# A hybrid decoder layer on one core: the order of input loads, weight casts and forget gates in the first stage

## The chip, the core and the metric

The kernel runs on one core of one Trainium2 chip. The metric is the device time of one execution in microseconds (us), as the median of several runs. The profile is of one further execution.

## The reference

One layer of a hybrid decoder works on 2,048 prompt tokens and 32 sample tokens (eight sequences of four), of width 1,024, in float32:

```python
h = rmsnorm(x, g_pre)
proj = h @ w_in                    # q, k, v, z_a, r, glu, z_b, g_a, g_b
log_a = log_sigmoid(r @ w_a_up + b_a_up) / 16
o, s_new = gla_chunked(q, k, v, log_a, s0)        # S_t = diag(alpha_t) S_{t-1} + k_t^T v_t ; o_t = q_t S_t
y_a = (rmsnorm(o, g_gla) * silu(z_a)) @ w_a_out
u = glu_a * sigmoid(glu_g)
cv = silu(layernorm(causal_dwconv(u, width 31)))
y_b = (cv * silu(z_b)) @ w_b_out
x = x + (sigmoid(g_a) * y_a + sigmoid(g_b) * y_b) @ w_o
x = x + sigmoid(x @ w_pg) * (p @ w_pe)
y = rmsnorm(x, g_final)
```

The recurrence has four heads with keys of 128 and values of 256; r has rank 16. The states of the recurrence and the last 30 rows of the convolution are outputs as well.

## The kernel before

Every large product is computed from two float16 halves of each operand, high and low, with three matmuls per tile of 128 rows (mm3, lines 266 to 268). So each weight that comes from memory is cast twice: ACT writes the high half (Copy with a scale), DVE the low half (what is left). These pairs are the **weights' casts**: lines 217 and 218 in load_w, lines 307 and 308 in gate_w.

The kernel goes through these stages.

1. **The input.** There are 17 token tiles: 16 of 128 prompt tokens and one with the 32 sample tokens. load_x (line 332) loads a tile into a buffer of the tag x, of which there are eight; eight loads are asked for at once (line 339), the others when the loop comes to them and a buffer is free. The loop over P0_GROUPS (line 342) takes the tiles in groups of 1, 1, 2, 4, 4, 4 and 1. For a group, ACT squares and sums each tile (line 350), rsqrt computes the root by three Newton steps (lines 175 to 191 and 198; on DVE for the first two groups, on GpSimd, called POOL here, for the other five), DVE scales the tiles (line 357), PE transposes them (line 366), and ACT and DVE copy the high and the low half to xT (lines 370 and 371). xT holds h transposed, in eight tiles of 2,080 columns.
2. **Early gates.** With groups 0, 1, 4 and 5, gate_w loads the weights of one block of 128 columns of z_b each (line 355), in two pieces through the tag stf, of which there are two buffers.
3. **The forget gates.** r is projected (line 398) and split (lines 400 and 401). For each of the four heads, PE projects r up (line 408); ACT takes the absolute value (409) and DVE adds the bias (410), in five pieces of the 2,080 columns; then come Exp (412) and Ln (413) on ACT, minimum and difference (414) and the running sum (415) on DVE, and a store to b_d (416). For heads 1 to 3 the steps from 412 on are of lower priority. The tags e and la have two buffers each.
4. **Recurrence and convolution**, interleaved: the generator gla_head makes 36 steps (four heads, nine segments of tokens), and conv_channels(c) is called ahead of the steps in CPOS, for c = 0 ahead of the first. Its weights and those of the heads come through load_w, which has four staging buffers (st) and eight for the results (w). The gate projections (gate_proj, line 311: 24 blocks of columns by five blocks of 416 tokens) have the lowest priority, FILL: they fill PE where nothing else is ready. Their results go by ob (line 318, 320) to memory.
5. **The rest**: the branch outputs with w_a_out and w_b_out (line 605 on), w_o, the per-layer embedding, the last norm.

What sets the order. The program is written as straight code with priorities. A scheduler places the instructions of each engine in one fixed order, by priority and by a model of when each one's inputs are there; the engines then work through their orders. issue_after(i) adds one constraint: what is traced within it stands behind i in the order of i's engine. It is no wait for i's end. wdma (line 203) uses it to place loads of weights behind the load of the last x tile so far. Loads go by SP's queue (dma, line 107), stores by POOL's (store, line 110).

Tiles of a pool take fixed places in the on-chip memory, and a tile of a later pool that lies on the place of an earlier one waits for that one's last use. The pools pg (forget gates) and p0 (x) lie one behind the other from byte 123,040 of each partition; pg ends at 172,352 with the second buffer of la (8,320 bytes). When both are done, p2 (recurrence) begins at byte 123,040 as well and is 45,408 bytes long; p1 (convolution) lies at the other end and begins at byte 172,160 with the first buffer of ue. The pool fill (gates) begins at byte 213,728.

## Time and profile before

| | |
|---|---|
| median of 3 runs | 2454.31 us (2452.01 to 2458.31) |
| the profiled execution, its own time | 2464.93 us |
| its span | 2463.2 us |
| mean granted clock of PE | 0.983 |
| PE busy in 0 to 100 us | 51.98 us |
| PE busy in 100 to 200 us | 90.26 us |
| PE busy in 200 to 300 us | 97.93 us |

How to read it. PE is the matrix engine (PEld its weight loads), DVE the vector engine, ACT the scalar engine, POOL GpSimd; SPq are the instructions by which SP issues loads. Times are in us from the start of the span unless marked ns. A row of a timeline has start, duration, engine, line of the kernel, operation, tiles with their shapes, and how many instructions were merged; in brackets stands the engine's idle time ahead of it and what ended it. A row of busy time by window has, for each engine, busy us and in parentheses the number of instructions, and then the granted clock of PE, the mean busy share of the DMA engines and the rate in GB/s. A row of a line's instructions has the shortest, median and longest duration in ns and the first and last start in us.

### The profile page before, as it was taken

The page shows a single profiled execution, that of the slowest core. Times are in us where ns is not written, and L with a number is a line of the kernel's source. Part 1 is how long each engine was busy: PE and PEld are TensorE (multiplying, and loading weights), DVE is VectorE, ACT ScalarE, POOL GpSimd, SP SyncE. Part 2 cuts the span into 40 slices and gives each one's busy share as a digit, 9 for nine tenths or more (in the row PEclk, how much of TensorE's full clock was granted, in tenths as well). Part 3 has the DMA queues.
Part 4 walks back from the last instruction along what each step waited for, and adds up shares of the span by engine and source line. Part 5 has one row for each costly group of instructions (what it writes and reads, how often), then busy time and mean ns, then how long its engine had stood idle before and what let it go on. Part 6 is the DMA issues. An engine that isn't in the chain of part 4 may idle for free.

```text
span 2463.2 us, 43458 instructions
## 1 busy us (share of the span) xinstructions
PE 2336.9 (95%) x16909; PEld 1467.2 (60%) x16909; DVE 1676.1 (68%) x3779; ACT 859.7 (35%) x2043; POOL 451.7 (18%) x1023
## 2 busy tenths in 40 slices
PE   5589999998899999999999989999999998999997
PEld 3245565654456655556655556655999997444544
DVE  6476897496594695594775784654577878865666
ACT  6462123323123324123224223443234334423454
POOL 2011203211112122222122222121000000111333
PEclk9799999999999999999999999999999999999999
DMA  5441201104112113211113130245355445742322
GB/s 182 108 145 32 66 27 61 43 10 125 45 48 63 35 33 111 62 36 51 34 51 94 63 81 29 58 123 166 96 128 130 114 111 181 188 142 89 101 80 73
DMA packets 195942, 210.04 MB, mean 85 GB/s; under 512 B 39323, under 2 KB 167641, under 8 KB 194200
## 3 DMA queue, kind: packets, MB, share of 16 engines
q1 hardware_dynamic: 172104, 133.85, 20.9%
q0 software_dynamic: 23632, 73.42, 8.4%
q8 instruction: 132, 2.16, 0.4%
q14 instruction: 74, 0.61, 0.1%
HBM read 138.33 MB, written 69.72 MB: 84 GB/s over the span
## 4 chain that ended last, share of the span: by engine, by line
PE 74%; DVE 8%; DMA 7%; issue 4%; POOL 4%; ACT 2%; SPq 1%; DVEq 0%; POOLq 0%; ACTq 0%
PE mm L266 13%; PE mm L267 13%; PE mm L268 13%; PE fl L266 6%; PE fl L267 6%; PE fl L268 6%; PE mm L685 4%; PE fl L685 3%; POOL ms L198 1%; DVE acc L504 1%; DMA st<-in_w_in 1%; PE sm L1028 1%; PE sm L1030 1%; PE sm L1029 1%; DMA st<-in_w_pg 1%
## 5 line engine op out<-in xcount | busy, mean ns | idle before, releaser
L266 PE MATMUL mm<-xT,w 128*128 128x416 f16 (+2 forms) x1216 | 362.5, 303 | 4.1 <-DVE zz L932 4.1
L268 PE MATMUL mm<-xT,w 128*128 128x416 f16 (+2 forms) x1216 | 362.4, 303 | 1.0 <-DVE w L218 1.0
L267 PE MATMUL mm<-xT,w 128*128 128x416 f16 (+2 forms) x1216 | 362.3, 303 | 0.0
L266 PE MATMUL fl<-xT,wf 128*128 128x416 f16 x960 | 329.9, 344 | 13.2 <-DVE ob L320 11.7
L267 PE MATMUL fl<-xT,wf 128*128 128x416 f16 x960 | 329.8, 344 | 0.0
L268 PE MATMUL fl<-xT,wf 128*128 128x416 f16 x960 | 329.6, 343 | 0.0
L504 DVE SCALAR_TENSOR_TENSOR acc<-ue,kvec,acc 128x1025 f32<-128x1025 f32 (+1 forms) x232 | 293.9, 1294 | 0.0
L267 PEld LDWEIGHTS <-w 128*128 128x128 f16 x2496 | 243.3, 98 | 69.6 <-issue 11.0
L266 PEld LDWEIGHTS <-w 128*128 128x128 f16 x2496 | 243.4, 98 | 63.2 <-issue 5.5
L268 PEld LDWEIGHTS <-w 128*128 128x128 f16 x2496 | 243.3, 98 | 59.5 <-issue 2.5
L685 PEld LDWEIGHTS <-f 128*128 128x128 f16 x1356 | 132.4, 98 | 160.6 <-issue 6.7
L266 PE MATMUL mm<-w,xT 128*128 128x512 f16 x512 | 195.3, 382 | 0.0
L267 PE MATMUL mm<-w,xT 128*128 128x512 f16 x512 | 195.1, 381 | 0.0
L268 PE MATMUL mm<-w,xT 128*128 128x512 f16 x512 | 195.1, 381 | 0.0
L685 PE MATMUL mm<-wf,f 128*128 128x512 f16 (+1 forms) x780 | 180.2, 379 | 7.3 <-ACT f L658 4.3
L266 PE MATMUL fl<-bT,w 128*128 128x208 f16 x640 | 162.5, 254 | 2.0 <-ACT ob L318 2.0
L266 PE MATMUL mm<-aT,w 128*128 128x208 f16 x640 | 161.5, 253 | 2.4 <-DMA aT<-a_d 2.4
L267 PE MATMUL fl<-bT,w 128*128 128x208 f16 x640 | 162.6, 254 | 0.0
L268 PE MATMUL fl<-bT,w 128*128 128x208 f16 x640 | 162.5, 254 | 0.0
L268 PE MATMUL mm<-aT,w 128*128 128x208 f16 x640 | 161.5, 253 | 0.0
L267 PE MATMUL mm<-aT,w 128*128 128x208 f16 x640 | 161.5, 253 | 0.0
L504 DVE SCALAR_TENSOR_TENSOR acc<-acc,ksum 128x1024 f32<-128x1024 f32 x120 | 155.0, 1292 | 0.0
(277 smaller groups left out, 4061.6 us busy)
## 6 DMA issues: line engine op xcount, KB each, us to landing
x<-in_x_prompt SPq DMA_DIRECT2D x32, 512.0 KB, 6.0
stf<-in_w_in SPq DMA_DIRECT2D x48, 256.0 KB, 6.5
st<-in_w_in SPq DMA_DIRECT2D x24, 512.0 KB, 10.4
zz_d<-ob POOLq DMA_DIRECT2D x40, 208.0 KB, 2.8
ta_d<-ob POOLq DMA_DIRECT2D x40, 208.0 KB, 2.3
tb_d<-ob POOLq DMA_DIRECT2D x40, 208.0 KB, 2.6
cv<-cv_d SPq DMA_DIRECT2D x80, 104.0 KB, 2.1
zz<-zz_d SPq DMA_DIRECT2D x80, 104.0 KB, 2.2
```

The source lines that it names most:

```text
L198: E.tensor_scalar(out=x, in0=x, scalar1=scale, scalar2=EPS, op0=MULT, op1=ADD)
L266: PE.matmul(out, lhsT=lh, rhs=rh, start=(k == 0), stop=False)
L267: PE.matmul(out, lhsT=lh, rhs=rl, start=False, stop=False)
L268: PE.matmul(out, lhsT=ll, rhs=rh, start=False, stop=(k == nk - 1))
L504: V.scalar_tensor_tensor(out=out[:, 0:n], in0=src[:, j:j + n], scalar=w1[:, j:j + 1], in1=out[:, 0:n], op0=MULT, op1=ADD)
L685: PE.matmul(ps[:, c0:c0 + w], lhsT=F[fa][:, p == 2, k], rhs=W[fb][k // 2][:, p == 1, k % 2, c0:c0 + w], start=start and k + p == 0, stop=k ...
L1028: PE.matmul(po[:, c], lhsT=qe[:, cc], rhs=st_prev, start=True, stop=False)
L1029: PE.matmul(po[:, c], lhsT=att[:, c], rhs=v[:, c], start=first, stop=True)
L1030: PE.matmul(pu[:, c * DV:(c + 1) * DV], lhsT=kdT[:, cc], rhs=v[:, c], start=True, stop=True)
```

## The change

- The tag x has 13 buffers (XB) in place of eight, and 13 tiles are asked for at once. The taps of the convolution share the tag.
- The tags e and la have one buffer each in place of two. The pool pg gets 16,640 bytes shorter by this, and p0 20,480 bytes longer.
- rsqrt in the input's loop runs on DVE for all groups.
- A new function split_w makes the two casts of a weight, for load_w and gate_w. Once the input's loop has been traced (hold), it places them by issue_after behind the instructions in xcopies, each on its own engine. xcopies holds the latest copies to xT, and after head 0's gates have been traced, the last piece's instructions of lines 409 and 410 (before the change's numbering) of that head. All casts that are traced with hold set come after head 0, so these are behind its gates. The four early gates' casts are traced with hold not set.
- The weights of the second to fourth early gate are loaded by POOL's queue in place of SP's.

```diff
--- before.py
+++ after.py
@@ -73,11 +73,11 @@
 T_BUFS = [2, 2]
 LN_AT = 33
 R_TR = [0, 0, 0, 0, 0]
-P0_DVE = 2
 
 EARLY = {0: False, 1: False, 4: True, 5: True}
 GSEGS = [(i * 256, 256) for i in range(8)] + [(T, TD)]
 CPOS = [0, 1, 5, 9, 13, 18, 22, 27]
+XB = 13
 P0_GROUPS = [1, 1, 2, 4, 4, 4, 1]
 SU = 2.0 ** 6
 SR = 2.0 ** 3
@@ -161,7 +161,7 @@
             nc.gpsimd.memset(onesd, 1.0 / D)
 
     def conv_taps(pool):
-        taps = pool.tile([P, D], F32, tag="x", name="taps", bufs=8)[0:CW]
+        taps = pool.tile([P, D], F32, tag="x", name="taps", bufs=XB)[0:CW]
         dma(taps, A["w_dw"][0])
         pt = sm_tile()
         for k in range(KC):
@@ -198,7 +198,18 @@
         E.tensor_scalar(out=x, in0=x, scalar1=scale, scalar2=EPS, op0=MULT, op1=ADD)
         return newton(x, y, t, E)
 
-    xdma = [None]
+    xdma, hold = [None], [False]
+
+    xcopies = []
+
+    def split_w(hi, lo, st):
+
+        with ExitStack() as es:
+            if hold[0]:
+                for i in xcopies:
+                    es.enter_context(tc.issue_after(i.ins))
+            S.activation(hi, st, AF.Copy, scale=SW)
+            V.scalar_tensor_tensor(out=lo, in0=st, scalar=SW, in1=hi, op0=MULT, op1=SUB)
 
     def wdma(out, in_):
 
@@ -214,8 +225,7 @@
         st = wst.tile([P, nk, len(c0) * width], F32, tag="st", name="st")
         for i, c in enumerate(c0):
             wdma(st[:, :, i * width:(i + 1) * width], src[k0 * P:(k0 + nk) * P, c:c + width].rearrange("(k p) c -> p k c", p=P))
-        S.activation(w[:, 0], st, AF.Copy, scale=SW)
-        V.scalar_tensor_tensor(out=w[:, 1], in0=st, scalar=SW, in1=w[:, 0], op0=MULT, op1=SUB)
+        split_w(w[:, 0], w[:, 1], st)
         return w
 
     def load_forms(src, tiles, accum):
@@ -303,9 +313,8 @@
         for g in range(2):
             k0, k1 = 4 * g, 4 * g + 4
             st = fill.tile([P, 4, P], F32, tag="st", name="stf", bufs=2)
-            (dma if early_w else wdma)(st, w_in[k0 * P:k1 * P, base + c * P:base + (c + 1) * P].rearrange("(k p) c -> p k c", p=P))
-            S.activation(w[:, 0, k0:k1], st, AF.Copy, scale=SW)
-            V.scalar_tensor_tensor(out=w[:, 1, k0:k1], in0=st, scalar=SW, in1=w[:, 0, k0:k1], op0=MULT, op1=SUB)
+            (wdma if not early_w else store if c else dma)(st, w_in[k0 * P:k1 * P, base + c * P:base + (c + 1) * P].rearrange("(k p) c -> p k c", p=P))
+            split_w(w[:, 0, k0:k1], w[:, 1, k0:k1], st)
         return w
 
     def gate_proj(c, which, w):
@@ -331,12 +340,12 @@
 
         def load_x(i):
             src, r = x_rows(i)
-            t = p0.tile([P, D], F32, tag="x", name="x", bufs=8)
+            t = p0.tile([P, D], F32, tag="x", name="x", bufs=XB)
             loads[i] = (t, r, dma(t[0:r], src))
         load_x(0)
         dma(ident, A["c_ident"])
         small_vectors(p0)
-        for i in range(1, 8):
+        for i in range(1, XB):
             load_x(i)
         trs = []
         for gi, nt in enumerate(P0_GROUPS):
@@ -350,7 +359,7 @@
                 S.activation(sq[0:r], t[0:r], AF.Square, accum_out=ss[0:r, j:j + 1])
                 xt.append((t, r))
             r = xt[0][1]
-            rs = rsqrt(ss[0:r, 0:nt], nt, r, 1.0 / D, V if gi < P0_DVE else nc.gpsimd)
+            rs = rsqrt(ss[0:r, 0:nt], nt, r, 1.0 / D, V)
             if gi in EARLY:
                 early.append(gate_w(len(early), 0, EARLY[gi], True))
             for j, (t, r) in enumerate(xt):
@@ -367,10 +376,11 @@
                 trs.append(tr)
                 for k in range(k0, k0 + kk):
                     o = (k - k0) * n
-                    S.activation(xT[k][:, 0, a:a + n], pt[:, o:o + n], AF.Copy, scale=g_pre[:, k:k + 1])
-                    V.scalar_tensor_tensor(out=xT[k][:, 1, a:a + n], in0=pt[:, o:o + n], scalar=g_pre[:, k:k + 1],
-                                           in1=xT[k][:, 0, a:a + n], op0=MULT, op1=SUB)
-
+                    xcopies[:] = [S.activation(xT[k][:, 0, a:a + n], pt[:, o:o + n], AF.Copy, scale=g_pre[:, k:k + 1]),
+                                  V.scalar_tensor_tensor(out=xT[k][:, 1, a:a + n], in0=pt[:, o:o + n], scalar=g_pre[:, k:k + 1],
+                                                         in1=xT[k][:, 0, a:a + n], op0=MULT, op1=SUB)]
+
+        hold[0] = True
 
         reset = pg.tile([P, TT], F16, name="reset", bufs=1)
         nc.gpsimd.memset(reset, 1.0)
@@ -400,14 +410,16 @@
             S.activation(rh, ps[:, 0:n], AF.Copy, scale=mlo[:, 0:1])
             V.scalar_tensor_tensor(out=rT[:, a:a + n], in0=ps[:, 0:n], scalar=IS * SR, in1=rh, op0=MULT, op1=SUB)
         for h in range(NH):
-            e = pg.tile([P, TT], F32, tag="e", name="e")
-            la = pg.tile([P, TT], F32, tag="la", name="la")
+            e = pg.tile([P, TT], F32, tag="e", name="e", bufs=1)
+            la = pg.tile([P, TT], F32, tag="la", name="la", bufs=1)
             for a, n in SEGS:
                 ps = sm_tile()
                 for i in range(2):
                     PE.matmul(ps[:, 0:n], lhsT=wu[:, i, h * DK:(h + 1) * DK], rhs=rT[:, a:a + n], start=(i == 0), stop=(i == 1))
-                S.activation(e[:, a:a + n], ps[:, 0:n], AF.Abs, bias=b_up[:, h:h + 1], scale=1.0 / (SU * SR))
-                V.tensor_scalar(out=la[:, a:a + n], in0=ps[:, 0:n], scalar1=1.0 / (SU * SR), scalar2=b_up[:, h:h + 1], op0=MULT, op1=ADD)
+                es = [S.activation(e[:, a:a + n], ps[:, 0:n], AF.Abs, bias=b_up[:, h:h + 1], scale=1.0 / (SU * SR)),
+                      V.tensor_scalar(out=la[:, a:a + n], in0=ps[:, 0:n], scalar1=1.0 / (SU * SR), scalar2=b_up[:, h:h + 1], op0=MULT, op1=ADD)]
+                if h == 0:
+                    xcopies[:] = es
             with later(GATES if h else 0):
                 S.activation(e, e, AF.Exp, scale=-1.0)
                 S.activation(e, e, AF.Ln, bias=1.0)
```

## The prediction

> **What bounds the kernel now.** I read the page first, then the busy time by window, and then ACT's, SP's and DVE's rows in the windows where PE is idle.
>
> ```profile
> span 2463.2 us, 43458 instructions
> PE 2336.9 (95%) x16909; PEld 1467.2 (60%) x16909; DVE 1676.1 (68%) x3779; ACT 859.7 (35%) x2043; POOL 451.7 (18%) x1023
> ```
>
> PE is busy for 2336.9 of 2463.2 us, so what it does not do is 126.3 us in all. A change that leaves the matmuls as they are can gain from these 126.3 us and from matmuls that ran at a lowered clock, and from nothing else. The windows (busy time of PE, PEld, DVE, ACT, POOL, then the granted clock, the DMA share and GB/s) show where a large part lies:
>
> ```profile
> 20.00:30.00 10.00, 3.28 (x9) 1.35 (x9) 6.14 (x15) 4.90 (x13) 2.99 (x10) 1.00 0.49 164
> 50.00:60.00 10.00, 9.16 (x64) 4.54 (x63) 8.56 (x14) 8.04 (x16) 0.78 (x1) 1.00 0.60 226
> 70.00:80.00 10.00, 3.65 (x16) 3.38 (x17) 6.31 (x9) 3.10 (x4) 0.62 (x1) 0.58 0.47 112
> 80.00:90.00 10.00, 0.60 (x2) 0.09 (x1) 2.95 (x4) 3.34 (x5) 0.00 (x0) 0.50 0.42 100
> 90.00:100.00 10.00, 6.17 (x23) 3.79 (x24) 3.69 (x6) 2.13 (x3) 0.00 (x0) 0.67 0.65 185
> 100.00:110.00 10.00, 7.58 (x40) 3.26 (x40) 5.67 (x13) 5.27 (x12) 0.00 (x0) 0.55 0.52 140
> 130.00:140.00 10.00, 8.38 (x48) 4.49 (x46) 10.00 (x6) 8.04 (x11) 1.08 (x2) 1.00 0.43 150
> 140.00:160.00 20.00, 14.74 (x81) 7.56 (x80) 13.49 (x17) 14.27 (x16) 2.15 (x4) 0.92 0.29 101
> ```
>
> From 70 to 110 PE, DVE and ACT are all mostly idle at once, which is the sign of a transfer that everybody waits for. ACT's own rows name it:
>
> ```profile
> 78.22 1.06 ACT L217 ACTIVATE w<-st 128x1024 f16<-128x1024 f32 x1 [3.77 <-DMA st<-in_w_in]
> 80.79 1.06 ACT L217 ACTIVATE w<-st 128x1024 f16<-128x1024 f32 x1 [1.52 <-DMA st<-in_w_in]
> 87.72 1.06 ACT L217 ACTIVATE w<-st 128x1024 f16<-128x1024 f32 x1 [5.87 <-DMA st<-in_w_in]
> 88.68 2.40 ACT L370 ACTIVATE xT<-sm,g_pre 128x512 f16<-128x512 f32 x4
> 97.88 1.06 ACT L217 ACTIVATE w<-st 128x1024 f16<-128x1024 f32 x1 [6.80 <-DMA st<-in_w_in]
> 100.74 1.06 ACT L217 ACTIVATE w<-st 128x1024 f16<-128x1024 f32 x1 [1.80 <-DMA st<-in_w_in]
> 101.70 1.82 ACT L370 ACTIVATE xT<-sm,g_pre 128x512 f16<-128x512 f32 x3
> ```
>
> ACT works its queue in order. The weight casts (L217) stand in it between the copies of the last token tiles (L370); each waits for its load, and the copies behind it, which have their data, wait too. PE then gets neither transposes released nor complete rows of xT. Upstream of that, SP's queue shows why the token tiles themselves come late:
>
> ```profile
> 19.63 12.73 SPq L108 DMA_DIRECT2D stf<-in_w_in  x4
> 35.24 0.82 SPq L108 DMA_DIRECT2D x<-in_x_prompt  x2
> 37.69 3.80 SPq L108 DMA_DIRECT2D stf<-in_w_in  x2
> 48.82 1.76 SPq L108 DMA_DIRECT2D x<-in_x_prompt  x4
> 61.20 0.33 SPq L108 DMA_DIRECT2D x<-in_x_sample  x1
> ```
>
> With eight buffers, the loads of later tiles stand behind early weight loads that wait for a staging buffer, and the last tile is asked for at 61.20 us. The whole start therefore is a chain of queues, and not work of any engine.
>
> **Part by part. 1: the casts behind the copies.** This removes no instruction. It takes the casts from between the copies, so the stall of 70 to 110 us goes. Its price: PE's busy time there is 3.65 + 0.60 + 6.17 + 7.58 = 18.00 of 40 us, so 22.0 idle; and with the granted clock of each row the 18.00 us are worth 3.65 x 0.58 + 0.60 x 0.50 + 6.17 x 0.67 + 7.58 x 0.55 = 10.7 us at full clock, so 7.3 more are lost. Together 29.3 us. The Trainium skill (TensorE: Matmul & The Clock Gate, Part 1) has the clock come back after one busy window of about 3.4 us. By it two returns would lose half of 3.4 us each, 3.4 in all in place of 7.3, and the sum below would be 24 in place of 28; this trace does not agree, since its grant stays near 0.6 over the 20 us from 90 to 110.
>
> What comes in the stall's place is the work that the copies need. From these rows (the copies to xT, the scaling of x, the early casts; then one rsqrt of a group on DVE):
>
> ```profile
> L371 DVE SCALAR_TENSOR_TENSOR xT<-sm,g_pre,xT x56: 244/476/752, 12.7 to 112.4; 128x512 f16<-128x512 f32 x24, 128x128 f16<-128x128 f32 x16, 128x256 f16<-128x256 f32 x8, 128x32 f16<-128x32 f32 x8
> L357 DVE TENSOR_SCALAR x<-x,rsq_y x17: 733/749/754, 10.0 to 78.4; 128x1024 f32<-128x1024 f32 x16, 32x1024 f32<-32x1024 f32 x1
> L308 DVE SCALAR_TENSOR_TENSOR wf<-stf,wf 128x512 f16<-128x512 f32 x8 | 5.5, 689 | 6.0 <-ACT wf L307 6.0
> ```
>
> ```profile
> 5.52 0.15 DVE L198 TENSOR_SCALAR ss<-ss 128x1 f32<-128x1 f32 x1
> ...
> 6.86 0.16 DVE L182 SCALAR_TENSOR_TENSOR rsq_y<-rsq_t,rsq_y 128x1 f32<-128x1 f32 x1
> ```
>
> The copies are 24 x 0.75 + 32 x up to 0.48, by the maximum and the median, at most 33 us; I take 27, since half of the small ones are near the minimum. The scaling is 17 x 0.749 = 12.7. The seven rsqrt are 1.5 us each (5.52 to 7.02), 10.5, of which five, 7.5 us, are new on DVE: the change moves them from POOL. The casts are 5.5. That is 56 us of DVE from 5.5 us on. With DVE's share of the window 50 to 60 (8.56 of 10), in which it did just this work with the data at hand, xT is complete at 5.5 + 56 / 0.856 = 71; with its share of 20 to 30 (6.14) at 97. I take 75, near the first, because after the change the tiles lie in SBUF ahead of their use. Before, the last copy began at 112.4, so about 37 us earlier. While the copies run PE loses what it lost in 50 to 60, 0.84 in 10, so about 1 us over the 13 us or so that the copies still need after 62. Part 1 nets 29.3 - 1 = 28 us.
>
> **2: thirteen tiles at once.** Without this, part 1 would only lead to the next wait, SP's. Five more loads go ahead of the first early weights in SP's queue. They delay head columns' first weights and the r weights by five issues and 2.6 MB; at the 226 GB/s of 50 to 60 that is 11.6 us for the first early gate. PE has transposes then, but the window 20 to 30 shows only 3.28 us of them. Bounds: a loss of the 3.3 us that PE did there, or a gain of the 6.7 that it was idle, because tiles no longer wait. I take nothing.
>
> **3: early weights 1 to 3 on POOL's queue.** They leave SP, where their waits held x (19.63 to 61.20). On POOL they wait for the two staging buffers, and behind them stand the stores of the gates' results (zz_d). POOL is rid of the rsqrt, so nothing else waits. The price is a store held for one cast; PE has two accumulators for that, so nothing is counted. The Trainium skill (DMA: Bandwidth & Descriptors, Issuing engines are not separate DMA queues) says that loads from another engine's queue share the same 16 DMA engines and save only the issue time; the rows cannot tell the two apart here, and what it would make of the time is the third rival.
>
> **4: one buffer for e and la.** Head 0's gates start at xT's end. Each further head now waits until the store of the one before has landed. The rows:
>
> ```profile
> L413 ACT ACT_TABLE_LOAD  x4: 1283/1283/1283, 122.5 to 158.9; - x4
> L413 ACT ACTIVATE e<-e x4: 1936/1937/1937, 123.8 to 160.2; 128x2080 f32<-128x2080 f32 x4
> L414 DVE SCALAR_TENSOR_TENSOR la<-la,e x4: 2302/2324/2326, 125.7 to 163.0; 128x2080 f32<-128x2080 f32 x4
> L415 DVE TENSOR_TENSOR_SCAN e<-reset,la x4: 4482/4485/4490, 128.8 to 166.9; 128x2080 f32<-128x2080 f16 x4
> 138.15 2.42 ACT L409 ACTIVATE e<-sm,vec 128x512 f32<-128x512 f32 x4 [1.93 <-DMA b_d<-e]
> ```
>
> Head 0's scan ended at 128.8 + 4.5 = 133.3, which is 20.7 after the last copy's end (112.4 + 0.2). Its store had landed at 138.15, 4.9 later. A head that starts then needs 2.7 for its five pieces of Abs, 1.94 for Exp (as for the Ln of this shape), 1.28 for the table, 1.94 for Ln, 2.32, 4.49, and 4.9 for its store: 19.6. So the last scan ends at 75 + 20.7 + 3 x 19.6 = 154.5, against 166.9 + 4.5 = 171.4 before: 17 us earlier, although xT was 37 earlier. The recurrence can't start before that scan, because its tiles lie where reset, e and la lie:
>
> ```profile
> 171.47 0.35 SPq L108 DMA_DIRECT2D lml<-in_c_lmask  x1
> L318 ACT ACTIVATE ob<-fl x120: 489/517/540, 49.7 to 1733.2; 128x416 f32<-128x416 f32 x120
> L111 POOL DMA_DIRECT2D a_d<-at x72: 706/740/826, 295.9 to 1694.6; - x72
> ```
>
> Does PE have work in the meantime? Yes: the gate projections, which are its filler to 1733.2, 39 us after the recurrence's last store. There is more of it now, since conv channel 0 needs no longer wait: its buffer ue began 192 bytes below the end of la's second buffer, and with pg shorter by 16,640 bytes it lies over buffers of the tag x alone. This channel's matmuls then also leave the recurrence's stage. The idle of 130 to 160 (1.62 + 5.26 = 6.9 us) may go or grow; I count it unchanged.
>
> **5: what is queued behind the held casts.** On ACT and DVE they now stand behind head 0's Abs and its bias add, and ahead of some of its Exp, of conv channel 0 and of all gates after the fourth:
>
> ```profile
> L218 DVE SCALAR_TENSOR_TENSOR w<-st,w 128x1024 f16<-128x1024 f32 x6 | 7.3, 1225 | 25.0 <-ACT w L217 25.0
> L217 ACT ACTIVATE w<-st 128x1024 f16<-128x1024 f32 x6 | 6.3, 1056 | 27.4 <-DMA st<-in_w_in 27.4
> st<-in_w_in SPq DMA_DIRECT2D x24, 512.0 KB, 10.4
> ```
>
> Four staging tiles are filled long before. The fifth and sixth cast wait for a buffer and a load, 10.4 us, in place of 27.4 for six. Between nothing and 10.4 + 7.3 us are added to head 0's chain; up to the 17 us of part 4 this costs PE nothing, as the four early gates are not held.
>
> **Sum.** 29.3 - 1 = 28 us off the profiled execution's 2464.93 us, to 2437. That execution is 10.6 above the median of the three runs, 2454.31; from the median it is **2426 us**.
>
> **Rivals.** *The recurrence becomes the bound* (0.13). PE's filler is then used up 28 us earlier, but the recurrence starts only 17 us earlier, or 7 if the two late casts lie on its way, and the next stage needs it. For it: the filler outlasted the recurrence by only 39 us (1733.2 against 1694.6), in which the next stage's weights were cast. Against it: conv channel 0 leaves that stage. Gain 7 to 17, say 12: 2442.
>
> *Slower: four heads in a row on one buffer* (0.12). If xT is complete only at 97 (DVE's share of 20 to 30) the last scan ends at 97 + 20.7 + 58.8 = 176.5, and with 17.7 us of casts and their waits at 194, 23 us after 171.4. It decides from the point where the recurrence starts later than before by more than the slack, that is from a head of over (171.4 - 95.7) / 3 = 25 us at my 75. Then the recurrence sets the end: up to 23 later, say 2467. Against it: DVE had the share of 0.86 as soon as tiles lay ready.
>
> *The transfers only change places* (0.07). Early weights 1 to 3 are 1.5 MB, the last tiles 1.7 MB; at 112 GB/s, the row of 70 to 80, together 29 us, so if they begin at 25 the last tile lands at 54. With xT complete at 75 it is wanted some 15 us before, at 60. If it lands at 70, xT is complete at 85 and PE loses these 10 us: 2436.
>
> *It doesn't do what it says* (0.06). The order is one of issue only; if xT's copies come to wait for PE's transposes behind other matmuls as long as they waited for loads, the stall stays: 2454.
>
> **How the numbers follow.** My forecast has 0.62. About 0.3%, 7.4 us, is what a measurement of this kernel can tell from no change. Faster by more: 0.62 + 0.13 + 0.07 = 0.82; the same 0.06; slower 0.12. The low end takes in the unknowns of the forecast that could go (6.9 of 130 to 160 and 6.7 of 20 to 30): 2426 - 13.6 = 2412, and 2410 rounded. The high end takes in the first and third rival with 12 - 5 = 7 us of gain, 2447, and 2449 with the runs' own spread; above it lie the slower rival and half of the last.
>
> **What would show it.** Right: the windows from 70 to 110 have PE above 9 at a clock of 1.00; no L217 stands between L370 rows; the last L371 begins at 71 to 80; x is asked for the last time before 45 us; lml is asked for at 150 to 165; ue is written before it. Wrong: L217 waits for loads ahead of L370 still; the last scan ends after 171; or PE is idle between 1690 and 1740 for more than the few us of before.

## The result and the profile after

| | before | after |
|---|---|---|
| median of 4 runs | 2453.16 us (2451.10 to 2458.31) | 2425.62 us (2421.11 to 2429.03) |
| the profiled execution | 2464.93 us | 2425.56 us |

The medians are 27.5 us apart; the ratio of all the runs is 0.9878 (95% interval 0.9858 to 0.9898), so the changed kernel is 25 to 35 us faster. The prediction said 2426. The line numbers below are the changed kernel's: casts 211 and 212, x scaled 366, copies to xT 379 and 380, Abs and bias of the forget gates 419 and 420, their scan 427, gate blocks' results ob 327 and 329, mm3 276 to 278.

The page's busy line of the changed kernel:

```profile
span 2423.8 us, 43460 instructions
PE 2331.2 (96%) x16909; PEld 1464.9 (60%) x16909; DVE 1680.7 (69%) x3834; ACT 858.2 (35%) x2043; POOL 438.5 (18%) x965
```

PE's idle time went from 126.3 to 2423.8 - 2331.2 = 92.6 us, 33.7 less, and its busy time fell by 5.7 at a higher clock. These 39.4 us between the two profiled executions are more than the 27.5 between the medians: the one of before is 11.8 us over its median of 2453.16. A part of that is one wait, which the list of PE's waits between 560 and 760 us shows for before (line, tile, what it waited for; us in all, times, longest):

```profile
PE sm L1052 <- DMA s<-in_state_gla: 9.7, 1, 9.7
```

In the changed kernel the same wait is 4.8. The windows of the changed kernel, for the stretches that the prediction quoted of before:

```profile
20.00:30.00 10.00, 6.29 (x26) 4.42 (x26) 9.71 (x31) 8.65 (x21) 1.71 (x2) 1.00 0.57 155
50.00:60.00 10.00, 6.47 (x32) 2.65 (x32) 2.60 (x6) 2.91 (x6) 0.75 (x1) 0.66 0.46 105
70.00:80.00 10.00, 9.45 (x69) 5.36 (x68) 8.21 (x14) 6.36 (x11) 0.56 (x1) 1.00 0.26 45
80.00:90.00 10.00, 10.00 (x88) 4.61 (x88) 5.77 (x15) 5.47 (x14) 0.54 (x1) 1.00 0.06 23
90.00:100.00 10.00, 10.00 (x59) 5.38 (x58) 7.25 (x9) 8.40 (x10) 0.54 (x1) 1.00 0.42 124
100.00:110.00 10.00, 9.29 (x53) 5.07 (x52) 6.23 (x4) 6.59 (x6) 0.00 (x0) 1.00 0.84 218
130.00:140.00 10.00, 9.50 (x55) 5.20 (x54) 5.28 (x5) 1.14 (x3) 1.62 (x3) 1.00 0.55 188
140.00:160.00 20.00, 15.45 (x88) 8.23 (x87) 12.99 (x12) 11.32 (x14) 2.70 (x5) 1.00 0.22 75
```

From 70 to 110 PE does 38.74 us of 40 at full clock, where it did 18.00 at 0.50 to 0.67. But a new hole stands at 50 to 60: 6.47 at a clock of 0.66, where it was 9.16 at 1.00. Taken together, the first 200 us of before and of after:

```profile
0.00:200.00 200.00, 142.23 (x802) 77.38 (x803) 111.43 (x197) 106.97 (x180) 31.73 (x95) 0.91 0.44 135
```

```profile
0.00:200.00 200.00, 160.94 (x948) 88.71 (x949) 121.51 (x259) 110.12 (x186) 22.72 (x42) 0.97 0.47 143
```

At full clock that is 142.23 x 0.91 = 129 us of work before and 160.94 x 0.97 = 156 after: the start has gained 27 us, by all parts of the change together. ACT's rows show the new hole:

```profile
51.70 0.63 ACT L211 ACTIVATE wf<-stf 128x512 f16<-128x512 f32 x1 [6.16 <-DMA stf<-in_w_in]
52.23 1.25 ACT L379 ACTIVATE xT<-sm,g_pre 128x512 f16<-128x512 f32 x2
58.88 0.63 ACT L211 ACTIVATE wf<-stf 128x512 f16<-128x512 f32 x1 [5.39 <-DMA stf<-in_w_in]
59.41 1.83 ACT L379 ACTIVATE xT<-sm,g_pre 128x512 f16<-128x512 f32 x3
84.02 0.28 ACT L379 ACTIVATE xT<-sm,g_pre 128x32 f16<-128x32 f32 x1
```

It is the same kind of wait as before, smaller: the casts of the early gates (wf) are not held, so they still stand between the copies and wait for their loads. The other rows that the prediction named, by line (count, then shortest, median and longest ns, first and last start), and then from SP's queue:

```profile
L380 DVE SCALAR_TENSOR_TENSOR xT<-sm,g_pre,xT x56: 242/478/751, 12.6 to 84.8; 128x512 f16<-128x512 f32 x24, 128x128 f16<-128x128 f32 x16, 128x256 f16<-128x256 f32 x8, 128x32 f16<-128x32 f32 x8
L427 DVE TENSOR_TENSOR_SCAN e<-reset,la x4: 4482/4488/4491, 107.9 to 175.2; 128x2080 f32<-128x2080 f16 x4
L327 ACT ACTIVATE ob<-fl x120: 491/517/542, 43.9 to 1698.3; 128x416 f32<-128x416 f32 x120
L111 POOL DMA_DIRECT2D a_d<-at x72: 708/733/798, 289.6 to 1659.1; - x72
```

```profile
27.40 1.18 SPq L108 DMA_DIRECT2D x<-in_x_sample  x1
28.63 15.12 SPq L108 DMA_DIRECT2D st<-in_w_in  x4
179.76 0.36 SPq L108 DMA_DIRECT2D lml<-in_c_lmask  x1
```

The last copy begins at 84.8, not 75, the last scan ends at 179.7, not 154.5, and lml is asked for 8 us **later** than before. Still the recurrence's last store is 35.5 us earlier (1659.1 against 1694.6). So the total came out while three numbers on the way to it did not.

### The profile page after: what moved, and what is told of

It is laid out like the page before. It is cut to its first block, busy times and chain, and to the rows that moved or that the text cites. A ratio compares the mean times of both kernels' runs of the same rounds, so it can differ in the third digit from the quotient of the medians.

```text
span 2423.8 us, 43460 instructions
## 1 busy us (share of the span) xinstructions
PE 2331.2 (96%) x16909; PEld 1464.9 (60%) x16909; DVE 1680.7 (69%) x3834; ACT 858.2 (35%) x2043; POOL 438.5 (18%) x965
## 4 chain that ended last, share of the span: by engine, by line
PE 74%; DMA 8%; DVE 6%; issue 5%; POOL 4%; ACT 2%; SPq 0%; DVEq 0%; POOLq 0%; ACTq 0%
PE mm L276 12%; PE mm L278 12%; PE mm L277 12%; PE mm L697 6%; PE fl L277 6%; PE fl L276 6%; PE fl L278 6%; PE fl L697 4%; DMA stf<-in_w_in 2%; DMA zz_d<-ob 1%; DVE acc L516 1%; PE sm L1040 1%; PE sm L1041 1%; PE sm L1042 1%; POOL ms L198 1%
## 5 line engine op out<-in xcount | busy, mean ns | idle before, releaser
L516 DVE SCALAR_TENSOR_TENSOR acc<-ue,kvec,acc 128x1025 f32<-128x1025 f32 (+1 forms) x232 | 292.0, 1276 | 0.0
L516 DVE SCALAR_TENSOR_TENSOR acc<-acc,ksum 128x1024 f32<-128x1024 f32 x120 | 153.0, 1275 | 0.0
```

The costliest lines, as they stand in the source:

```text
L516: V.scalar_tensor_tensor(out=out[:, 0:n], in0=src[:, j:j + n], scalar=w1[:, j:j + 1], in1=out[:, 0:n], op0=MULT, op1=ADD)
```

## The experiments

The theory after the result: casts that wait for loads ahead of copies are the whole loss; and the start of the recurrence sets nothing, as PE has gate blocks to do until 1698 either way. The rivals: the loads' order or the queue is what counts; or the heads' chain does. Each run stands beside runs of the kernel before on the same chip, in three groups: the first four, the next four, the last four.

| kernel | median, us | ratio to before (95%) |
|---|---|---|
| held casts alone | 2423.83 | 0.9874 (0.9860 to 0.9889) |
| changed kernel, no hold | 2433.59 | 0.9910 (0.9895 to 0.9924) |
| changed kernel, early weights on SP | 2443.70 | 0.9951 (0.9938 to 0.9965) |
| changed kernel, two early gates | 2418.82 | 0.9853 (0.9838 to 0.9867) |
| changed kernel, two buffers of e and la | 2425.67 | 0.9881 (0.9866 to 0.9897) |
| changed kernel, rsqrt on POOL | 2430.25 | 0.9901 (0.9886 to 0.9916) |
| held casts, two early gates | 2401.21 | 0.9785 (0.9770 to 0.9801) |
| two early gates and two buffers | **2390.47** | 0.9739 (0.9724 to 0.9753) |
| changed kernel, taps first | 2435.80 | 0.9928 (0.9912 to 0.9944) |
| two and two, taps first | 2424.45 | 0.9879 (0.9861 to 0.9898) |
| one early gate, two buffers | 2403.68 | 0.9794 (0.9776 to 0.9812) |
| two and two, no hold | 2430.61 | 0.9905 (0.9884 to 0.9926) |

### The held casts alone

The kernel before with split_w, xcopies and hold; against the changed kernel:

```diff
-XB = 13
+XB = 8
-            (wdma if not early_w else store if c else dma)(st, w_in[k0 * P:k1 * P, base + c * P:base + (c + 1) * P].rearrange("(k p) c -> p k c", p=P))
+            (dma if early_w else wdma)(st, w_in[k0 * P:k1 * P, base + c * P:base + (c + 1) * P].rearrange("(k p) c -> p k c", p=P))
-            rs = rsqrt(ss[0:r, 0:nt], nt, r, 1.0 / D, V)
+            rs = rsqrt(ss[0:r, 0:nt], nt, r, 1.0 / D, V if gi < P0_DVE else nc.gpsimd)
-            e = pg.tile([P, TT], F32, tag="e", name="e", bufs=1)
-            la = pg.tile([P, TT], F32, tag="la", name="la", bufs=1)
+            e = pg.tile([P, TT], F32, tag="e", name="e")
+            la = pg.tile([P, TT], F32, tag="la", name="la")
```

> The kernel before with part 1 alone: casts behind the copies and behind head 0's gates; eight buffers of x, two of e and la, rsqrt on POOL, early weights on SP. Theory (the casts between the copies were the loss, 28 us): the last copy to xT begins at about 80 in place of 112.4, no cast of a held weight stands between copies, and the time is 2424 to 2434, that is at least two thirds of the gain. Rival (the loads' order, so thirteen tiles at once, was the loss and the casts only wait where ACT had nothing else): the last copy stays after 95 and the time is over 2441, less than half of the gain.

2423.83 us, 31.1 under before and just under the theory's range: the held casts give the whole gain, with eight buffers. Its windows:

```profile
70.00:80.00 10.00, 9.40 (x63) 5.19 (x62) 8.09 (x15) 6.18 (x13) 1.63 (x3) 1.00 0.50 124
80.00:90.00 10.00, 10.00 (x87) 4.90 (x87) 5.33 (x13) 5.68 (x14) 0.54 (x1) 1.00 0.43 96
90.00:100.00 10.00, 10.00 (x59) 5.49 (x58) 9.26 (x12) 9.98 (x14) 0.54 (x1) 1.00 0.58 165
100.00:110.00 10.00, 9.39 (x52) 4.94 (x51) 8.19 (x5) 9.93 (x8) 0.00 (x0) 1.00 0.86 231
```

The last x is asked for at 61.45, as late as before, and the copies end all the same at 82.8. The loads' order was not what came next. Its first 200 us hold 162.95 x 0.98 = 160 us of work at full clock, 30 more than before.

### The rest without the held casts

```diff
-        hold[0] = True
```

> The changed kernel with part 1 alone undone: casts go where the scheduler puts them; thirteen tiles, one buffer of e and la, rsqrt on DVE, early weights on POOL stay. Theory (part 1 is the gain): casts stand between copies again, the last copy begins 10 to 30 us after the 84.0 of the changed kernel, and the time is 2440 to 2455. Rival (the thirteen tiles are the gain): the time stays at 2422 to 2430 although casts stand between copies, since their loads begin at 28 and have landed.

2433.59, between the two expectations; the last copy begins at 91.9. The other parts alone give 21 us, the held casts alone 31, and both together 27.5 (each against the runs of before beside it). The parts are substitutes. With 13 tiles asked for at once, the casts of load_w come to wait only 2.4 us in all in ACT's order, and those of the early gates 12.6.

### The early weights on SP's queue

```diff
-            (wdma if not early_w else store if c else dma)(st, w_in[k0 * P:k1 * P, base + c * P:base + (c + 1) * P].rearrange("(k p) c -> p k c", p=P))
+            (wdma if not early_w else dma)(st, w_in[k0 * P:k1 * P, base + c * P:base + (c + 1) * P].rearrange("(k p) c -> p k c", p=P))
```

> The changed kernel with the second to fourth early gate's weights loaded by SP's queue again. In the changed kernel ACT waits 13.2 us for these loads between copies, while the four loads of held weights (from 28.6) and the last x tiles are under way. Theory (all queues share the same engines, so POOL's queue gains nothing but issue time): the waits stay within 5 us of 13.2 and the time within 4 us of 2425.6. Rival (POOL's queue is needed so that x does not wait behind them on SP): x is asked for the last time over 10 us later than at 27.4, and the time is 2432 to 2445.

2443.70, 18 us more than the changed kernel (the profiled execution was the fastest of its runs, 2436.79). SP's queue in this kernel:

```profile
27.35 1.83 SPq L108 DMA_DIRECT2D stf<-in_w_in  x2
29.27 2.22 SPq L108 DMA_DIRECT2D x<-in_x_sample  x1
31.54 13.38 SPq L108 DMA_DIRECT2D st<-in_w_in  x4
45.03 7.14 SPq L108 DMA_DIRECT2D stf<-in_w_in  x2
```

x is not late at all (29.27). It is the early weights that are: the second pair stands behind the four st loads (4 x 512 KB), which take 13.38 us to issue. ACT waited for such loads 17.9 us in all, 15.1 of it at once. Neither side of the expectation had that. The Trainium skill (DMA: Bandwidth & Descriptors, Issuing engines are not separate DMA queues) says that issuing from several engines saves only the sequencer's time, which it calls usually small beside the transfer. That agrees with these rows, if this time is read as that of everything ahead in the same order, 13.38 us here; it is not small beside the 7.3 us that a load of stf takes from issue to landing in this run (the median of 48).

### Two early gates

```diff
-EARLY = {0: False, 1: False, 4: True, 5: True}
+EARLY = {0: False, 1: False}
```

> The changed kernel with two early gates in place of four: the third and fourth gate's weights are loaded and cast later, held like all others. Theory (a cast that waits for its load between copies is the remaining loss in the input's stage, 13.2 us of waits on ACT): the last copy begins at 70 to 77 in place of 84.0, and the time falls by 2 to 8 us, to 2418 to 2424. Rival (PE needs these gates as its filler while head 0's gates are pending): the last copy is earlier, but PE is idle longer between 60 and 100, and the time is 2428 to 2436.

2418.82, 6.8 less; the runs of the two kernels overlap (2417.01 to 2422.88 against 2421.11 to 2429.03), so this is at the edge of what they can tell. The last copy begins at 74.9, which is the 75 of the prediction, and PE has no hole from 40 to 80:

```profile
40.00:60.00 20.00, 20.00 (x134) 10.95 (x134) 18.32 (x49) 13.08 (x22) 1.12 (x2) 1.00 0.46 120
60.00:80.00 20.00, 20.00 (x162) 10.63 (x162) 12.63 (x25) 11.44 (x24) 1.08 (x2) 1.00 0.07 26
```

ACT waits 0.6 us for early weights here, where it was 13.2. So the last two early gates, whose casts the change leaves in place, are what made the copies ten us late; the edit takes their matmuls from this stretch as well, and the two were not taken apart. The ten us are not what the total gains by: from 100 to 160 PE does 48.88 us at a clock of 0.89, where the changed kernel does 50.08 at 1.00, and the first segment of the recurrence is stored at 293.8 against 290.4.

### Two buffers of e and la

```diff
-XB = 13
+XB = 9
-            e = pg.tile([P, TT], F32, tag="e", name="e", bufs=1)
-            la = pg.tile([P, TT], F32, tag="la", name="la", bufs=1)
+            e = pg.tile([P, TT], F32, tag="e", name="e")
+            la = pg.tile([P, TT], F32, tag="la", name="la")
```

> The changed kernel with nine x buffers and two buffers each of e and la, as before. Theory (the start of the recurrence costs nothing, since PE has gate blocks to do until the end either way): the heads' period falls from 22.4 to about 12.5 us, the last scan ends near 145 in place of 180, lml is asked for near 148, and still the time stays at 2425, at most 4 us less, by the idle of the window 140 to 160 (4.5 us in the changed kernel); the last x is asked for about 10 us later and the last copy stays within 3 us of 84. Rival (the price that the prediction put on one buffer is real, up to 23 us for 23 us of later start): the recurrence begins 30 us earlier and the kernel gains 15 to 25 us, 2400 to 2410.

2425.67, the changed kernel's time to 0.1 us, with this row:

```profile
145.90 0.35 SPq L108 DMA_DIRECT2D lml<-in_c_lmask  x1
```

The recurrence may begin 34 us earlier, and nothing comes of it. The lead melts: the first segment of the recurrence is stored 18 us earlier (272.2 against 290.4), the sixth 8, the last 7, and the kernels end together.

### The roots on POOL

```diff
-            rs = rsqrt(ss[0:r, 0:nt], nt, r, 1.0 / D, V)
+            rs = rsqrt(ss[0:r, 0:nt], nt, r, 1.0 / D, V if gi < 2 else nc.gpsimd)
```

> The changed kernel with the last five rsqrt back on POOL. A rsqrt takes about 4.5 us there (before) against 1.5 on DVE, and POOL's early weight loads stand in the same order. Theory (neither DVE's 7.5 us nor POOL's 22 us limits the copies, the early casts' waits do): last copy within 3 us of 84, time 2421 to 2429. Rival A (DVE's work is the path, as the prediction's sum has it): last copy 7 us earlier, 2418 or so. Rival B (the rsqrt's place matters because it holds the early loads in POOL's queue): those loads 3 us later each, last copy 90, 2432 or more.

2430.25, 4.6 more than both the changed kernel and its neighbour in the same group. The last copy begins at 84.7, unchanged, as the theory said; the time is just outside its range. The roots on DVE are worth some 4.6 us by this (the runs of the two kernels of the group do not overlap), and where they gain them wasn't found.

### Held casts and two early gates

On the kernel with the held casts alone:

```diff
-EARLY = {0: False, 1: False, 4: True, 5: True}
+EARLY = {0: False, 1: False}
```

> The kernel before with the held casts alone, and only the first two early gates. Theory (casts that wait for loads between the copies are the whole loss, and with two early gates SP's queue holds no x behind staging buffers): x last asked for before 40, last copy near 75 as with two early gates in the changed kernel, lml near 140; 2411 to 2417, below both the held casts alone (2424) and the changed kernel with two early gates (2419). Rival (13 buffers, rsqrt on DVE or POOL's queue do have a share in the 2419): x is late for want of buffers, last copy over 80, 2420 to 2426.

2401.21, less than either side expected. And the theory's reason fails: the last x is asked for at 58.47 and the last copy begins at 83.0, no earlier than with four early gates (82.6). The end of the copies is not what this kernel gains by.

### Two early gates and two buffers

The edits of "two early gates" and of "two buffers" together, on the changed kernel:

```diff
-EARLY = {0: False, 1: False, 4: True, 5: True}
+EARLY = {0: False, 1: False}
-XB = 13
+XB = 9
-            e = pg.tile([P, TT], F32, tag="e", name="e", bufs=1)
-            la = pg.tile([P, TT], F32, tag="la", name="la", bufs=1)
+            e = pg.tile([P, TT], F32, tag="e", name="e")
+            la = pg.tile([P, TT], F32, tag="la", name="la")
```

> The changed kernel with two early gates, nine x buffers and two buffers each of e and la. Theory (after the last copy the heads' single buffers leave PE idle from 100 to 160, 11.1 us of 60 in the changed kernel with two early gates; with two buffers the held casts alone left 8.2 of 60 there): last copy near 75, last scan near 137, lml near 142, PE over 51 of 60 from 100 to 160, 2414 to 2418. Rival (an earlier recurrence is worth its 40 us in part): 2400 to 2410. Rival (it moves nothing, as the blocks of the gates fill in either way): 2419.

2390.47, the best of the study and under all three expectations: 65.6 us under before, 35 under the changed kernel. By itself one of its two edits gave 6.8 and the other nothing. Where it comes from is read by counting. A segment of the recurrence ends with two stores to a_d; a gate block ends with one ob. The times are those of the second store:

| stored segment | before: at us, blocks done | after | two buffers | two and two |
|---|---|---|---|---|
| 1st | 298.2, 22 | 290.4, 22 | 272.2, 22 | 271.9, 18 |
| 2nd | 402.5, 29 | 375.6, 28 | 371.4, 29 | 353.6, 25 |
| 28th | 1463.5, 91 | 1425.5, 91 | 1417.9, 91 | 1397.3, 88 |
| 29th | 1495.2, 92 | 1458.8, 92 | 1450.6, 92 | 1417.3, 88 |
| 36th | 1694.6, 114 | 1659.1, 113 | 1652.1, 113 | 1620.9, 111 |
| end of span | 2463.2, 120 | 2423.8, 120 | 2423.3, 120 | 2393.8, 120 |

A block is 24 matmuls that start 0.176 us apart, 4.2 us. At the second segment the best kernel is 17.8 us ahead of the one with two buffers alone, which is just the four blocks (16.9 us) that it has not done yet. With each block still missing counted as 4.22 us (24 x 0.176), it is ahead by 0.9 us there, by 7.9 at the 28th segment, 16.4 at the 29th, 22.8 at the 36th and 29.5 at the end. So the gain is made late and in several places. From the 29th segment on, the four blocks cost the best kernel 3.8 us in place of 16.9: it does 23 in 203.6 us to the 36th where the other does 21 in 201.5, and then 9 in 772.9 where the other does 7 in 771.2.

The largest single step is from the 28th to the 29th segment, 20.0 us in place of 32.7. There the kernel with two buffers alone has this wait of PE (the list of PE's waits, 1370 to 1620):

```profile
PE sm L1042 <- DVE state L1047: 6.4, 1, 6.4
```

and DVE's rows name what stands ahead of the state's update (L1047):

```profile
1431.75 0.38 DVE L539 TENSOR_TENSOR s<-cv 128x208 f32<-128x208 f32 x1 [8.79 <-DMA cv<-cv_d]
...
1433.03 0.47 DVE L1047 SCALAR_TENSOR_TENSOR state<-state,ein,sm 128x256 f32<-128x256 f32 x1
```

This is the wait of the first stage again, on another engine: a sum of the convolution's norm waits 8.79 us for its load (cv), and the update of the recurrence's state, for which PE waits, stands behind it in DVE's order. It is no want of gate blocks, since 28 of 120 are still to be done at the 29th segment. DVE has this wait, 7.1 to 13.2 us long, in every kernel here that has done 91 blocks at the 28th segment, and in none of the five that have done 88 (those with both fewer early gates and two buffers). In the best kernel no gate weights are loaded in the 15 us ahead of these loads of cv, and the first eight take 3.81 us to issue; in the other two such loads begin 4.5 us ahead of them, and the eight take 9.79. That this is how the missing blocks and the wait hang together is argued and not shown.

From 1400 to 1600 the two kernels have, first with two buffers alone, then with both edits:

```profile
1400.00:1600.00 200.00, 186.68 (x1467) 112.49 (x1466) 112.46 (x384) 86.19 (x244) 45.56 (x129) 0.96 0.25 76
```

```profile
1400.00:1600.00 200.00, 197.78 (x1499) 118.83 (x1498) 104.61 (x365) 86.73 (x244) 42.17 (x132) 0.99 0.27 80
```

Over the spans, 29.5 us apart, 16.6 are idle time of PE (6.3 of it between the 28th and the 29th segment) and 12.9 busy time: the same matmuls at a mean clock of 0.993 in place of 0.987. Both edits are needed to have the early blocks undone: with two early gates but one buffer, the first segment comes at 293.8 and again with 22 blocks done. The kernel with the held casts and two early gates (2401.21) fits this count: it has two buffers too, has done 18 blocks at the first segment and 88 at the 28th and 29th, and is behind the best kernel from the start, with 15.55 us of PE at 0.83 from 60 to 80 where the best has 19.42 at 1.00.

### The taps first

For the prediction's claim on channel 0: the taps are made ahead of the heads, so that ue need not wait for them.

```diff
         hold[0] = True
+        conv_taps(p0)
...
-        conv_taps(p0)
```

> The changed kernel with the convolution's taps made ahead of the heads in place of behind them, so that ue no longer waits for the taps tile that lies under it. Theory (PE has filler either way, so it does not matter which of its work comes first): ue is written some 30 us before 167, PE's idle time from 100 to 200 falls by at most the 10.8 us that it is in the changed kernel and more likely by 3, time 2420 to 2426. Rival (the prediction's: channel 0's matmuls leave the recurrence's stage, which shortens the end by what they take, about 10 us): 2412 to 2416.

2435.80, 10 us **slower** than the changed kernel; neither side expected that. The first block of ue is written at 114.1, 55 us earlier. But then its convolution follows on DVE (acc, L516, 1.28 us each) and stands between the pieces of the heads:

```profile
171.18 1.28 DVE L516 SCALAR_TENSOR_TENSOR acc<-ue,kvec,acc 128x1024 f32<-128x1024 f32 x1
172.38 0.58 DVE L329 SCALAR_TENSOR_TENSOR ob<-ob,fl 128x416 f32<-128x416 f32 x1
172.88 0.24 DVE L421 TENSOR_SCALAR la<-sm,vec 128x32 f32<-128x32 f32 x1
173.04 1.28 DVE L516 SCALAR_TENSOR_TENSOR acc<-ue,kvec,acc 128x1025 f32<-128x1025 f32 x1
```

Its windows:

```profile
160.00:180.00 20.00, 16.22 (x82) 8.19 (x81) 20.00 (x23) 11.45 (x16) 5.45 (x11) 0.91 0.21 63
180.00:200.00 20.00, 11.68 (x50) 5.57 (x48) 19.99 (x23) 3.11 (x7) 5.83 (x12) 0.74 0.54 180
```

DVE is busy for 39.99 of 40 us and has become the bound; PE waits 12.1 us for DVE's part of ob and loses 12.1 of 40.

### The taps first, on the best kernel

The same edit on "two and two":

```diff
         hold[0] = True
+        conv_taps(p0)
...
-        conv_taps(p0)
```

> The kernel with two early gates, nine x buffers and two buffers each of e and la, with the taps made ahead of the heads. Theory: as in the changed kernel, 0 to 6 us less than 2390.5, since PE's idle time from 100 to 160 is 9.3 us there and half of it is a wait of the gate blocks for DVE's part of ob, which channel 0's matmuls can fill. Rival (channel 0 early takes the place that the gate blocks had and its DVE work delays the heads): 2392 to 2400.

2424.45, 34 us more, which neither side expected. Another wait this time:

```profile
81.77 1.03 PE L168 MATMUL sm<-ident,taps 31*128 31x31 f32 x8 [9.08 <-DMA taps<-in_w_dw]
```

The load of the taps stands in SP's order behind the st and stf loads and is asked for at 70.89 only; PE stands still for it. From 60 to 100 PE does 30.33 us at a clock of 0.83, 25 at full clock, where the best kernel does 39.42 at 1.00. The spans are 32.2 us apart, 16.0 of it idle time and 16.2 busy time at a lower clock (0.985). That stretch accounts for 14 of these, the wait of 9.1 among them; where the others come from isn't settled.

### One early gate

On "two and two":

```diff
-EARLY = {0: False, 1: False}
+EARLY = {0: False}
```

> Nine x buffers and two buffers each of e and la, with the first early gate alone. Theory (two are enough to fill PE until the next weights are cast, one is not: a gate is five blocks of 24 matmuls of 0.34 us, 41 us): the copies end by 73, but PE is idle for 10 to 25 us more between 60 and 110, time 2398 to 2412. Rival (every early gate costs by itself, as 28 us from four to two might be read): about 2376.

2403.68, within the range, but its reason was mis-sized: a gate's five blocks are 5 x 4.2 = 21 us and not 41, since matmuls overlap and their durations don't add up. PE did 39.02 of 40 us from 60 to 100, so no idle of 10 to 25 us arose there either. At the first segment it has done 18 blocks, as many as with two. Fewer early gates are not better without end.

### The best kernel without the held casts

```diff
-        hold[0] = True
```

> The kernel with two early gates, nine x buffers and two buffers each of e and la, with no cast held. Theory (the casts of load_w go between the copies again and wait there for their loads): last copy 5 to 12 us later than with them held, PE idle for 5 to 10 us more before 100, time 2396 to 2402, as the same step cost 8 us in the changed kernel. Rival (with two early gates their loads come in time and the held casts do nothing): 2390 within 2.

2430.61: in this kernel the held casts are worth 40 us, far more than either side expected. The stall of the kernel before is back:

```profile
60.00:80.00 20.00, 5.87 (x30) 1.44 (x29) 7.62 (x17) 6.87 (x9) 0.00 (x0) 0.61 0.59 157
80.00:100.00 20.00, 9.86 (x42) 6.87 (x42) 13.68 (x24) 9.47 (x13) 0.54 (x1) 0.62 0.63 164
```

with 22.2 us of ACT's time in waits of the casts of w for st. With the casts held PE does 39.42 us in these 40, at full clock.

## Why the prediction was right, and where it was wrong

**Part 1, the stall.** Right, and the best supported. The 28 us are there three times: the start gained 27 us of work at full clock (30 with the held casts alone); the held casts alone gave 31 us of time; and taking them out of the best kernel brings the stall back at 39.42 - 15.73 = 23.7 idle and 15.73 x 0.39 = 6.1 of clock, 29.8, where the spans differ by 33.8. The way of pricing (idle time, and busy time by the granted clock) held. On the clock the Trainium skill (TensorE: Matmul & The Clock Gate, Part 1) has it back after one busy window of some 3.4 us; in the windows of this last kernel it was 0.61 and 0.62 over 40 us with 15.73 us of work in small pieces. Whether one of these was the sustained busy window that the page asks for isn't shown, so here too the measured grant decides.

**xT complete at 75.** Wrong: 85. The step that failed is the sentence that takes the casts from between the copies. It takes only the held ones. The prediction counted the early casts as 5.5 us of DVE and not as waits, and they waited 13.2 us on ACT. With two early gates the last copy began at 74.9. The sum itself had 71, and 75 was a choice between 71 and 97, so this agreement is in part luck; but the work was sized well: in that kernel DVE was busy with copies for 27.8 us where 27 were taken, and with scaling for 11.9 where 12.7 were.

**Part 2, "without this, part 1 would only lead to the next wait, SP's".** Wrong. Without it the gain is the same. x came late and still in time.

**Part 3, nothing counted.** The size was off on both halves: POOL's queue is worth 18 us in the changed kernel, and the roots on DVE, which the prediction booked as 7.5 us more work, bring 4.6. What was missed for the queue is that with x no longer in front, the four st loads go ahead of the early weights.

**Part 4, the heads.** The period was (175.2 - 107.9) / 3 = 22.4 us and not 19.6, so the last scan came 25 us after its forecast, 10.0 of them from the copies, 8.4 from three periods and 6.7 from casts and waits between the last copy and the first scan (22.9 us, 16.2 before), which lies within the bounds of part 5 (0 to 17.7). Channel 0 did not start early: ue is first written at 166.82, after kvec at 166.45, because the taps lie under it. And where it was made to start early, it cost time.

**The rivals.** The slower one's condition came true: the recurrence started later than before. Its price did not. The kernel with two buffers shows it, 34 us earlier and no faster. The term that fails is "then the recurrence sets the end": PE sets it, with blocks to do until 1698. This holds with four early gates; with two, the same two buffers are worth 28 us (2418.82 against 2390.47). The prediction's own sign of being wrong, a last scan after 171, came true as well (179.7), and the time came out all the same, since the sign hung on that price. *The recurrence becomes the bound* did not occur for the same reason. *The transfers only change places* came true in part: x was asked for early (27.4), the early weights waited in its place (13.2 us, where these waits were 5.6 before), and xT was complete at 85, as this rival had it; but its loss of 10 us did not show. *Doesn't do what it says* is excluded by the windows.

So 2426 came from one right term and from terms counted at nothing. Of these the chain of copies and heads was later than forecast at no cost, and part 3 brought a gain that hides in substitutes: with the held casts in place the other parts together are worth nothing (2423.83 against 2425.62). In the same way the new hole at 50 to 60, 9.16 - 6.47 x 0.66 = 4.9 us, which was not forecast, nearly met the 6.29 - 3.28 = 3.0 us gained at 20 to 30, which were taken as nothing. That the total fits to 0.4 us is luck; that it lies near rests on part 1, which the runs bear out.

## What to carry to other kernels

When casts or copies share an engine's order, ask of each one which load it waits for and what stands behind it: holding those whose load is late cost nothing and gave the whole gain, and the ones that were left showed up at once as the next hole. The same question, asked of DVE's order 1,300 us later, finds a wait of 8.8 us that stops PE for 6.4. Work that fills PE is a stock: four blocks left undone at the start cost 3.8 us from the 29th segment on in place of 16.9. Parts of a change that clear the same wait don't add up, so take each out and put each in alone.

## What the runs showed of the hardware that wasn't expected

Idle time of PE can cost more than itself. Between the best kernel and that with two buffers alone, 16.6 us of idle time go with 12.9 us of busy time; with the taps first, 16.0 with 16.2. The windows of the kernel with two buffers alone show the clock low where PE waited 6.4 us, and full after it:

```profile
1420.00:1440.00 20.00, 13.58 (x71) 8.08 (x70) 7.13 (x29) 5.04 (x17) 0.57 (x3) 0.83 0.48 124
1440.00:1460.00 20.00, 20.00 (x181) 13.54 (x180) 10.76 (x44) 7.73 (x25) 4.31 (x14) 1.00 0.07 25
```

Its rows show the size of it. Matmuls of 128x512 start 0.22 us apart ahead of the wait and 0.43 us apart behind it:

```profile
1426.54 0.38 PE L278 MATMUL mm<-w,xT 128*128 128x512 f16 x1
1426.76 0.38 PE L276 MATMUL mm<-w,xT 128*128 128x512 f16 x1
1433.56 1.22 PE L1042 MATMUL sm<-v,kdT 128*128 128x256 f32 x2 [6.42 <-DVE state L1047]
1434.57 0.63 PE L277 MATMUL mm<-w,xT 128*128 128x512 f16 x1
1435.00 0.63 PE L278 MATMUL mm<-w,xT 128*128 128x512 f16 x1
```

By 1437.87 they are 0.22 us apart again, or less than 4.5 us after the wait; at half pace that is an estimate of at most 2.2 us lost behind 6.4 us of waiting. So this hole is only a small part of the 12.9. It is no fixed rate: the changed kernel with two early gates and that with two buffers have the same idle time, 89.7 us, and 8.1 us between their busy times. That all of a busy difference comes from holes is argued and not shown.
